# An encoder's dilated-attention mixer: wide transposes for keys and queries, and a seven-product unit in four of its six projection pairs

## The chip, the cores and the metric

The kernel runs on one core of a Trainium2 chip. The metric is the device time of one execution in microseconds, the median of three runs. TensorE (PE) multiplies matrices; VectorE (DVE), ScalarE (ACT) and GpSimd (POOL) do the elementwise work; SyncE (SP) issues most transfers.

## The reference

A bidirectional encoder of two layers over 256 positions of width 2048, all in float32. Each layer is a token mixer and a gated MLP with a depthwise convolution. The first layer's mixer is grouped-query attention. The second layer's mixer, which the change touches, is this (shortened):

```python
def mixer_b(h, w_qkv, w_o, rel_bias):
    qkv = (h @ w_qkv).reshape(b, s, n_g, 3, hg, HEAD_DIM)      # 3 groups, q/k/v, 8 heads of 128
    for g, (window, dil) in enumerate(((128, 1), (512, 4), (2048, 16))):
        o, lz = dilated_group(qkv[:, :, g, 0], qkv[:, :, g, 1], qkv[:, :, g, 2],
                              rel_bias[:, g * hg:(g + 1) * hg], window, dil)
        ...                                 # softmax(q k^T / sqrt(128) + bias) v in the window
    wts = softmax(stack(log_zs), axis=0)    # the groups share the weight of each position
    y = concatenate([wts[g] * outs[g] for g in range(3)], axis=2)
    return y @ w_o
```

So there are 18 projections of 256 x 2048 by 2048 x 512: three groups, each with keys, queries and values, in two halves of four heads.

## The kernel before

**Products.** A weight matrix is packed in blocks of 512 columns and in four chunks of 512 rows. Every float32 product is three TensorE products of parts in the format float32r: high by high, high by low, low by high. `feed` handles one chunk: it loads two weight tiles of 512 KB through SyncE's queue, ScalarE rounds each to a high part (line 144), VectorE takes the difference as the low part (line 145), and TensorE does 24 products of 128 x 128 by 128 x 512 (lines 132 to 134) into two accumulators, one for each 128 positions. `project` feeds the four chunks. There are four buffers for high and for low parts, and these two operations are issued ahead of other work (`tc.high_priority(offset=AHEAD)`).

**The unit.** `fast_unit` takes one chunk for two column blocks at once. Two chunks by plain `feed` are 48 products. The unit treats them as a 2 x 2 by 2 x 2 block product by Strassen's scheme (in Winograd's form): seven block products of 2 x 3 matmuls, 42 in all (lines 186 to 188). It needs sums of weight tiles (line 178, in place), roundings and differences of seven tiles (lines 179, 180), four PSUM tiles besides the four accumulators, sums of the activations' blocks prepared before (`sums_begun`, `sums_made`: adds, differences, one rounding), and a fold of the partial results afterwards (a copy on ScalarE, eight adds and subtractions on VectorE). The gated MLP uses it in `up_pair` for four pairs of a gate and a value block of each layer, in the order `UP_ORDER`: three chunks of the gate side, the unit, three chunks of the value side.

**The second mixer.** For each half `hf` and group `g` the loop projects keys, then queries; then, for the half, the three value blocks. The rest runs beside the projections as generators. `start` puts one into the list `pending`, which `step` resumes once in each half chunk, first come first served; generators in the list `beside` are resumed at the other places. `k_gen` and `s_gen` write the projected keys and queries, scaled, to SBUF (`evac_scaled`, line 489) and turn them so that the head dimension lies on the partitions: `heads_T_dve` does this with 16 transposes of 32 x 256 elements on VectorE (`block_T`, line 386). For group 0 the result is split into high and low parts. Then come four score steps: products, bias, maximum, exponential. `value_stage` turns the probabilities and multiplies by the values; `quad_T` there makes one wide VectorE transpose within 32 x 32 blocks (line 377), and `quad_move` or `quad_place` carries the 16 blocks to their places, on GpSimd (lines 381 and 398) or ScalarE (line 396).

**Order.** The text gives priorities. A scheduler at compile time puts the instructions in each engine's queue, and each engine then works through its queue in order.

Of the kernel before, what the change touches and what calls it, by code (L numbers as in the profile page):

```python
# [14 lines left out]
P = 128  # L15
D = 2048
NT = 256
# [7 lines left out]
AHEAD = 60  # L25
UP = 2, 4, 6, 8
UP_ORDER = (1, 0), (2, 0), (3, 0), (0, None), (1, 1), (2, 1), (3, 1)
NWARM = 11
# [5 lines left out]
def tile_encoder(ctx: ExitStack, tc: tile.TileContext, x, xT, w_a, w_ao, q_gain, k_gain, w_b, w_bo,  # L34
# [355 lines left out]

    def quad_place(o, quad, i0, i1):
        for i in range(i0, i1):
            q, c = QC[i]
            dst, src = o[32 * c:32 * c + 32, :, 32 * q:32 * q + 32], quad[32 * q:32 * q + 32, c]
            if i % 2:
                nc.scalar.activation(dst, src, AF.Copy)
            else:
                nc.gpsimd.tensor_copy(dst, src)  # L398

    def late_transpose(hT, n, g, pool, tag, new_quad):  # L400
# [5 lines left out]
        if n < 3:  # L406
            quad = new_quad()
            for m in range(2):
                quad_T(quad, slice(m, 8, 2), h[:, m, n * 512:(n + 1) * 512])
            yield  # L410
            o = wide_tile(pool, tag)
            for i in range(0, 16, 8):
                quad_place(o, quad, i, i + 8)
# [72 lines left out]
    def evac_scaled(pool, accs, rstd, bufs=2):  # L486
# [3 lines left out]
        return o  # L490

    def ffn(l, hT, ss_in, cw, g_next, last, side=None):
        with tc.tile_pool(name=nm("fpool"), bufs=1) as fp:
# [32 lines left out]
            def folds():  # L526
                return [fp.tile([P, 2, 512], F32, tag=t, name=nm("fold")) for t in ("stg", "st")]

            def new_us():
# [139 lines left out]
            picks = {}  # L669

            def sums(kg, at, r, st):
                yield from sums_begun(kg, r, st)
                sums_made(kg, at, st)

            def sums_begun(kg, r, st, wait=0):
                for _ in range(wait):
                    yield
                hts = [hT[4 * kg + j][:2] for j in range(4)]
                for j, (hi, lo) in enumerate(hts):
                    with tc.issue_after(newest[0].ins):  # L680
                        nc.vector.tensor_tensor(r[:, j], hi.bitcast(F32), lo.bitcast(F32), ALU.add)
                    if j == 1:
                        yield
                v = r.rearrange("p (b j) (m t) -> p b j m t", b=2, m=2)
                st = st.rearrange("p i (j t) -> p i j t", j=2)
                a11, a21, a12, a22 = v[:, 0, :, 0], v[:, 0, :, 1], v[:, 1, :, 0], v[:, 1, :, 1]
                yield
                for o, x, y in ((0, a21, a22), (2, a21, a11), (1, a11, st[:, 0]), (3, a12, st[:, 1])):
                    nc.vector.tensor_tensor(st[:, o], x, y, ALU.subtract)
                yield  # L690

            def sums_made(kg, at, st):
                hts = [hT[4 * kg + j][:2] for j in range(4)]
                own = [pair_slot(at + 2 * i, [P, 4, 2, P], F32R, "s") for i in range(2)]
                split_in_order(*own, st.rearrange("p i (j t) -> p i j t", j=2))
                pick = {q: tuple(tuple(hts[b + j][i][:, m * P:(m + 1) * P] for j in range(2)) for i in range(2))
                        for q, b, m in ((1, 0, 0), (2, 2, 0), (4, 2, 1))}
                for q, i in ((5, 0), (6, 1), (7, 2), (3, 3)):
                    pick[q] = own[0][:, i], own[1][:, i]
                picks[kg] = pick  # L700

            def up_pair(p, order, gate_done):
                (a2, a4), (a3, a8) = new_acc(), new_acc()
                acc, begun = {2: a2, 3: a3, 4: a4, 8: a8}, set()
                sides, ns = ((a2, a4), (a3, a8)), (p, NPAIR + p)
                tt = nc.vector.tensor_tensor
                for i, (kg, side) in enumerate(order):
                    later = {s for _, s in order[i + 1:]}
                    if side is None:
                        acc.update({q: ps_tile() for q in (1, 5, 6, 7)})  # L710
                        end = [q for q, s in ((1, None), (5, None), (6, None), (7, None), (2, 0), (4, 0), (3, 1))
                               if not later & {None, s}]
                        fast_unit(acc, picks[kg], *(w_up[l][n, kg] for n in ns), begun, end, None)
                    else:
                        mine = ((2, 4), (3, 8))[side]
                        feed(sides[side], hT, kg, w_up[l][ns[side], kg], not begun.issuperset(mine),
                             not later & {side, None}, begun=[m for m in range(2) if mine[m] in begun])
                        begun.update(mine)
                    if 0 in begun or not begun >= {1, 2} or later & {0, None}:
                        continue  # L720
                    begun.add(0)
                    a, t = junk(), fp.tile([P, 2, 512], F32, tag="st", name=nm("fold"))
                    v, w = t[:, 0], t[:, 1]
                    nc.scalar.activation(a, acc[1], AF.Copy)
                    with tc.issue_after(newest[0].ins):
                        tt(v, acc[6], a, ALU.subtract)
                        tt(w, acc[7], v, ALU.add)
                        tt(a2, a2, a, ALU.add)
                        tt(a4, a4, w, ALU.subtract)
                    gate_done((a2, a4))  # L730
                    tt(v, acc[5], v, ALU.add)
                    tt(w, acc[5], w, ALU.add)
                tt(a3, a3, v, ALU.add)
                tt(a8, a8, w, ALU.add)
                return a3, a8

            kgs = list(range(4))
            ready = set()
            for hf, (p0, p1) in enumerate(HALVES):
# [5 lines left out]
                for p in range(p0, p1):  # L745
# [12 lines left out]

                    first = partial(sums, 0, 16, cg, cv)
                    if p == p0 and hf == 1:  # L760
                        sums_made(0, 16, early[1])
                    if p == 0:
                        va = project2(w_up[l], 0, NPAIR, hT, kgs, 1, gate_done, None, (), [first])
                    elif p in UP:
                        va = up_pair(p, UP_ORDER, gate_done)
# [92 lines left out]
                if hf == 0:  # L858
                    for ns in (0, 1), (2, 3):
                        if ns[0] == 2:  # L860
                            early = [fp.tile([P, 4, NT], F32, tag=t, name=nm(t)) for t in ("cg", "cv")]
                            start(sums_begun(0, *early, 4))
                        pair(wd, ns, slots, both[0] + both[3] + [(4, 0)] + f0 + [(4, 1), (5, 0)] + f1 + [(5, 1)], spot, folds,
# [383 lines left out]
    def mixer_b(hT, ss_in):  # L1247
        with tc.tile_pool(name="bpool", bufs=1) as bp:
# [14 lines left out]
            def biases(hf, g):  # L1263
# [12 lines left out]
                return [bt[:, None, i, ::-1].to_broadcast([P, 2, P]) for i in range(4)]  # L1276

            cw, turn = load_taps(1)
            allp = slice(None)
            for hf in range(2):  # L1280
# [4 lines left out]
                e = small.tile([P, 3, 8], F32, tag="e", name=nm("e"))  # L1285

                def k_gen(accs, kT):
                    ks = evac_scaled(bp, accs, rstd)
                    yield
                    yield  # L1290
                    yield from heads_T_dve(kT, ks, bp, "vl")

                def s_gen(g, accs, kT, bts, nmx=nmx, lsum=lsum, nmv=nmv, probs=probs, e=e):
                    qs = evac_scaled(bp, accs, rstd)
                    qT = pair_tile(bp, [P, 4, NT], "qT", 1, g > 0)
                    yield
                    yield
                    yield from heads_T_dve(qT, qs, bp, "vl")
                    W = NT if g == 0 else P
# [42 lines left out]
                def value_stage(hf=hf, probs=probs, e=e, vs=vs):  # L1342
# [17 lines left out]
                    def place(quad, n):  # L1360
                        o = wide_tile(bp, ("kTh", "kTl", "qTh", "qTl")[n])
                        if hf == 1 and n > 1:
                            quad_place(o, quad, 0, 16)
                        else:
                            quad_move(o, quad)
# [81 lines left out]
            def own(kg):  # L1447
                return pair_tile(bp, [P, 4, NT], "qT" if kg else "kT")

            def tmp():  # L1450
                return bp.tile([P, 4, NT], F32, tag="pT", name=nm("tmp"), bufs=2)

# [98 lines left out]
```

## Time and profile before

| | |
|---|---|
| median of three runs | 2230.33 us (2229.9 to 2230.64) |
| profiled execution | 2230.45 us, span 2228.6 us |
| TensorE busy | 2214.0 us, 9957 matmuls |
| VectorE, ScalarE, GpSimd busy | 1834.4, 1474.9, 481.0 us |
| keys, queries and values of the second mixer | 966.3 to 1382.4 us of the span |
| one projection of it | about 22 to 25 us |

All times in profile rows are microseconds from the start of the span unless they are marked otherwise. In the timeline a row is: start, duration, engine, line, operation, tiles written and read, count, and in brackets the idle time before it with what ended it. In a group row the count is followed by busy time, the mean of one in nanoseconds, and the idle time before them. In the table by stretch each engine has its busy time and its number of instructions; PEclk is the granted TensorE clock. Matmuls overlap, so the pace is the distance between their starts. The stages of the second mixer begin at 966.3 (keys, half 0, group 0), 988.0 (queries), 1011.2, 1035.6 (group 1), 1058.1, 1081.2 (group 2), 1103.5 (values), and for half 1 at 1173.9, 1199.5, 1221.2, 1245.2, 1267.7, 1290.8 and 1313.1.

### The profile page before, as it was taken

Reading aid. Unit: us, or ns where it says so; the run is one execution under the profiler, and the core shown is the slowest. Engines: PE = TensorE matmul, PEld = TensorE weight load, DVE = VectorE, ACT = ScalarE, POOL = GpSimd, SP = SyncE. Lnnn points to the kernel's source line nnn. Section 1 sums busy time; section 2 is a strip of 40 time slices with the busy share of each in tenths; the row PEclk is TensorE's granted clock in tenths of the full one; section 3 lists DMA queues with packets and bytes.
Section 4 is the critical chain, followed back from the end, with each engine's and each line's share of the span. In section 5 each row is a group of like instructions: output and inputs, shape, how many; then the busy total and the mean of one; then the engine's idle time right before and its main releaser. Section 6 shows DMA issues by size and latency. Waiting matters only on the chain.

```text
span 2228.6 us, 28901 instructions
## 1 busy us (share of the span) xinstructions
PE 2214.0 (99%) x9957; PEld 1833.5 (82%) x9957; DVE 1834.4 (82%) x2385; ACT 1474.9 (66%) x2214; POOL 481.0 (22%) x697
## 2 busy tenths in 40 slices
PE   9999999999999999999999999999999999999998
PEld 7888888888888888888888888888888888888887
DVE  6877669899897887968886878588798998879887
ACT  7667677787457777665455456566777865678764
POOL 3343222321002221040053006003222300112211
PEclk9999999999999999999999999999999999999999
DMA  8565655656656566665556565656555656656654
GB/s 302 193 211 188 217 189 188 201 189 196 204 182 221 184 206 197 198 189 197 187 185 199 178 192 170 205 184 213 189 192 196 198 198 198 214 164 217 222 194 142
DMA packets 126179, 439.59 MB, mean 197 GB/s; under 512 B 14408, under 2 KB 18248, under 8 KB 126032
## 3 DMA queue, kind: packets, MB, share of 16 engines
q1 hardware_dynamic: 123056, 429.05, 58.4%
q0 software_dynamic: 2688, 8.39, 1.5%
q8 instruction: 78, 1.28, 0.2%
q14 instruction: 69, 0.57, 0.1%
q10 hardware_dynamic: 288, 0.30, 0.0%
HBM read 432.34 MB, written 5.34 MB: 196 GB/s over the span
## 4 chain that ended last, share of the span: by engine, by line
PE 53%; DVE 1%; issue 1%; POOL 1%; DMA 1%; ACT 0%; POOLq 0%; DVEq 0%; ACTq 0%
PE acc L133 15%; PE acc L134 15%; PE acc L132 15%; PE ps L187 1%; PE ps L186 1%; PE ps L188 1%; PE acc L187 1%; PE acc L186 1%; PE acc L188 1%; DMA raw<-in_w_b_dram 1%; DVE wl L145 1%; DVE tT L386 1%; POOL wide L398 0%; PE ps L1394 0%; PE ps L339 0%
## 5 line engine op out<-in xcount | busy, mean ns | idle before, releaser
L145 DVE TENSOR_TENSOR wl<-raw,wh 128x1024 fp32r<-128x1024 f32 (+1 forms) x716 | 878.6, 1236 | 250.9 <-ACT wh L144 244.4
L144 ACT ACTIVATE wh<-raw 128x1024 fp32r<-128x1024 f32 (+1 forms) x716 | 745.4, 1047 | 411.3 <-PE acc L134 309.0
L133 PE MATMUL acc<-wl,xh 128*128 128x512 f32 x2048 | 798.7, 390 | 1.8 <-DVE wl L145 1.7
L132 PE MATMUL acc<-wh,xh 128*128 128x512 f32 x2048 | 799.0, 390 | 0.4 <-ACT wh L144 0.4
L134 PE MATMUL acc<-wh,xh 128*128 128x512 f32 x2048 | 797.0, 389 | 0.0
L133 PEld LDWEIGHTS acc<-wl,xh 128*128 128x128 f32 x2048 | 384.7, 188 | 84.4 <-DVE wl L145 6.2
L132 PEld LDWEIGHTS acc<-wh,xh 128*128 128x128 f32 x2048 | 384.7, 188 | 79.9 <-ACT wh L144 0.9
L134 PEld LDWEIGHTS acc<-wh,xh 128*128 128x128 f32 x2048 | 384.5, 188 | 79.4
L561 POOL COPY u<-quad 32x256 f32<-32x256 f32 x352 | 235.0, 668 | 704.7 <-DVE quad L377 686.7
L133 PE MATMUL acc<-wl,a 128*128 128x512 f32 x720 | 280.5, 390 | 0.7 <-DVE wl L145 0.7
L132 PE MATMUL acc<-wh,a 128*128 128x512 f32 x720 | 280.9, 390 | 0.0
L134 PE MATMUL acc<-wh,a 128*128 128x512 f32 x720 | 280.1, 389 | 0.0
L179 ACT ACTIVATE wh<-raw 128x1024 fp32r<-128x1024 f32 x112 | 118.9, 1061 | 108.9 <-PE acc L134 92.1
L561 ACT ACTIVATE u<-quad 32x256 f32<-32x256 f32 x352 | 147.9, 420 | 22.0 <-DVE quad L377 17.5
L133 PEld LDWEIGHTS acc<-wl,a 128*128 128x128 f32 x720 | 135.2, 188 | 29.1 <-DVE wl L145 1.7
L134 PEld LDWEIGHTS acc<-wh,a 128*128 128x128 f32 x720 | 135.1, 188 | 28.2 <-DVE a L328 0.2
L132 PEld LDWEIGHTS acc<-wh,a 128*128 128x128 f32 x720 | 135.2, 188 | 27.6
L180 DVE TENSOR_TENSOR wl<-raw,wh 128x1024 fp32r<-128x1024 f32 x112 | 133.7, 1219 | 4.3 <-ACT wh L179 3.5
L381 POOL COPY wide<-quad 32x256 f32<-32x256 f32 x133 | 89.8, 675 | 169.3 <-DVE quad L377 159.8
L489 ACT ACTIVATE stg<-acc,rstd 128x512 f32<-128x512 f32 x122 | 82.1, 683 | 33.2 <-PE acc L134 25.3
L398 POOL COPY wide<-quad 32x256 f32<-32x256 f32 x88 | 53.2, 605 | 234.6 <-DVE quad L377 167.5
L549 DVE SCALAR_TENSOR_TENSOR cg<-u,cw,cg 128x256 f32<-128x256 f32 x176 | 79.3, 501 | 0.1
(310 smaller groups left out, 2256.7 us busy)
## 6 DMA issues: line engine op xcount, KB each, us to landing
raw<-in_w_up_dram SPq DMA_DIRECT2D x352, 512.0 KB, 4.6
raw<-in_w_down_dram SPq DMA_DIRECT2D x176, 512.0 KB, 4.6
raw<-in_w_b_dram SPq DMA_DIRECT2D x144, 512.0 KB, 4.4
raw<-in_w_bo_dram SPq DMA_DIRECT2D x48, 512.0 KB, 4.3
raw<-in_w_a_dram SPq DMA_DIRECT2D x40, 512.0 KB, 4.9
raw<-in_w_ao_dram SPq DMA_DIRECT2D x32, 512.0 KB, 4.6
raw<-in_w_a_dram SPq DMA_DIRECT2D x16, 256.0 KB, 5.8
there<-quad POOLq DMA_DIRECT2D x6, 512.0 KB, 3.8
```

What stands on the lines that cost most here:

```text
L132: nc.tensor.matmul(accs[m], xh, wh[:, j, :], start=st, stop=False)
L133: nc.tensor.matmul(accs[m], xh, wl[:, j, :], start=False, stop=False)
L134: nc.tensor.matmul(accs[m], xl, wh[:, j, :], start=False, stop=sp)
L144: nc.scalar.activation(wh[:, c], r[:, c], AF.Copy)
L145: newest[0] = nc.vector.tensor_tensor(wl[:, c], r[:, c], wh[:, c].bitcast(F32), ALU.subtract)
L179: nc.scalar.activation(wh, r, AF.Copy)
L180: newest[0] = nc.vector.tensor_tensor(wl, r, wh.bitcast(F32), ALU.subtract)
L381: nc.gpsimd.tensor_copy(o[32 * c:32 * c + 32, :, 32 * q:32 * q + 32], quad[32 * q:32 * q + 32, c])
L398: nc.gpsimd.tensor_copy(dst, src)
L489: evac[0] = nc.scalar.activation(o[:, m, :], accs[m], AF.Copy, scale=rstd[:, m:m + 1])
L549: nc.vector.scalar_tensor_tensor(cj, halves(flat[:, j, o:o + NT])[:, ::-1], tap(n, j, i), cj, ALU.mult, ALU.add)
L561: put(u[32 * c:32 * c + 32, :, :, 32 * q:32 * q + 32], quad[32 * q:32 * q + 32, c].rearrange("p (j m) t -> p j m t", m=2))
```

## The change

Keys and queries of all six pairs are turned by two wide transposes on VectorE and 16 block moves, six of them on GpSimd and ten on ScalarE (`heads`), in place of 16 block transposes on VectorE. In four pairs, groups 1 and 2 of both halves, the key and the query projection become one `up_pair` of six plain chunks and one unit for chunk 0. Three of them use `UP_ORDER`; half 1, group 1 uses `MIX_ORDER`, in which two query chunks come before the unit and one after it. The sums of chunk 0 are prepared in each half beside the query projection of group 0. The key generator of such a pair starts when the unit has been folded, and is resumed from `beside`. During a pair, each third weight tile is loaded into another idle buffer, as the MLP does. The routines `sums`, `sums_begun`, `sums_made` and `up_pair` move out of `ffn` and take their operands as arguments.

```diff
+MIX = (0, 1), (0, 2), (1, 1), (1, 2)
+MIX_ORDER = (1, 0), (2, 0), (3, 0), (1, 1), (2, 1), (0, None), (3, 1)
+EVEN, HEADS_POOL = range(0, 16, 2), range(0, 16, 3)
...
-    def quad_place(o, quad, i0, i1):
-        for i in range(i0, i1):
+    def quad_place(o, quad, which, pool):
+        for i in which:
             q, c = QC[i]
             dst, src = o[32 * c:32 * c + 32, :, 32 * q:32 * q + 32], quad[32 * q:32 * q + 32, c]
-            if i % 2:
+            if i in pool:
+                nc.gpsimd.tensor_copy(dst, src)
+            else:
                 nc.scalar.activation(dst, src, AF.Copy)
-            else:
-                nc.gpsimd.tensor_copy(dst, src)
...
+    def up_pair(w, ns, lhs, order, picks, junk, fold_tile, first_done):
...
+                def heads(o, s):
+                    hi, lo = o
+                    t = hi if lo is None else bp.tile([P, 4, NT], F32, tag="vl", name=nm("tT"))
+                    tv, quad = t.rearrange("p j (m t) -> p (j m) t", m=2), quad_tile(bp, "pT", 2)
+                    for m in range(2):
+                        quad_T(quad, slice(m, 8, 2), s[:, m])
+                    quad_place(tv, quad, HEADS_POOL, HEADS_POOL)
+                    yield
+                    quad_place(tv, quad, [i for i in range(16) if i not in HEADS_POOL], ())
+                    if lo is not None:
+                        yield
+                        yield
+                        split(hi, lo, t)
+
                 def k_gen(accs, kT):
                     ks = evac_scaled(bp, accs, rstd)
                     yield
-                    yield
-                    yield from heads_T_dve(kT, ks, bp, "vl")
+                    yield from heads(kT, ks)
...
                     qT = pair_tile(bp, [P, 4, NT], "qT", 1, g > 0)
                     yield
-                    yield
-                    yield from heads_T_dve(qT, qs, bp, "vl")
+                    yield from heads(qT, qs)
+                    if g > 0:
+                        yield
+                        yield
...
                 for g in range(3):
                     bts = biases(hf, g)
-                    ka = project(w_b, 6 * g + 2 + hf, hT, kgs)
+                    ns = 6 * g + 2 + hf, 6 * g + hf
+                    if (hf, g) in MIX:
+                        kTs = []
+
+                        def k_done(accs, g=g, kTs=kTs):
+                            kTs.append(pair_tile(bp, [P, 4, NT], "kT", 1, g > 0))
+                            gen = k_gen(accs, kTs[0])
+                            next(gen)
+                            beside.append(gen)
+
+                        extra[0] = ((hpool, ["a0", "a1"]), (hpool, ["a6", "a7"]), (bp, ["e0", "e1"]))[hf * g]
+                        qa = up_pair(w_b, ns, hT, MIX_ORDER if (hf, g) == (1, 1) else UP_ORDER, picks, junk, fold_tile, k_done)
+                        extra[0] = None
+                        start(s_gen(g, qa, kTs[0], bts))
+                        continue
+                    ka = project(w_b, ns[0], hT, kgs)
                     kT = pair_tile(bp, [P, 4, NT], "kT", 1, g > 0)
                     start(k_gen(ka, kT))
-                    start(s_gen(g, project(w_b, 6 * g + hf, hT, kgs), kT, bts))
+                    if g == 0:
+                        beside.append(sums(hT, 0, 20, tmp(), tmp(), picks))
+                    start(s_gen(g, project(w_b, ns[1], hT, kgs), kT, bts))
```

More of the change, by code (lines that the diff above doesn't have):

```diff
@@ L412, in late_transpose @@
             for i in range(0, 16, 8):
-                quad_place(o, quad, i, i + 8)
+                quad_place(o, quad, range(i, i + 8), EVEN)
                 yield
@@ new lines, in sums_made @@
+    def sums_made(lhs, kg, at, st, picks):
+        own = [pair_slot(at + 2 * i, [P, 4, 2, P], F32R, "s") for i in range(2)]
+        split_in_order(*own, st.rearrange("p i (j t) -> p i j t", j=2))
+        pick = {q: tuple(tuple(lhs[4 * kg + b + j][i][:, m * P:(m + 1) * P] for j in range(2)) for i in range(2))
+                for q, b, m in ((1, 0, 0), (2, 2, 0), (4, 2, 1))}
+        for q, i in ((5, 0), (6, 1), (7, 2), (3, 3)):
+            pick[q] = own[0][:, i], own[1][:, i]
+        picks[kg] = pick
@@ new lines, in sums @@
+    def sums(lhs, kg, at, r, st, picks):
+        yield from sums_begun(lhs, kg, r, st)
+        sums_made(lhs, kg, at, st, picks)
+    def up_pair(w, ns, lhs, order, picks, junk, fold_tile, first_done):
+        (a2, a4), (a3, a8) = new_acc(), new_acc()
+        acc, begun = {2: a2, 3: a3, 4: a4, 8: a8}, set()
+        sides = (a2, a4), (a3, a8)
+        tt = nc.vector.tensor_tensor
+        for i, (kg, side) in enumerate(order):
+            later = {s for _, s in order[i + 1:]}
+            if side is None:
+                acc.update({q: ps_tile() for q in (1, 5, 6, 7)})
+                end = [q for q, s in ((1, None), (5, None), (6, None), (7, None), (2, 0), (4, 0), (3, 1))
+                       if not later & {None, s}]
+                fast_unit(acc, picks[kg], w[ns[0], kg], w[ns[1], kg], begun, end, None)
+            else:
+                mine = ((2, 4), (3, 8))[side]
+                feed(sides[side], lhs, kg, w[ns[side], kg], not begun.issuperset(mine),
+                     not later & {side, None}, begun=[m for m in range(2) if mine[m] in begun])
+                begun.update(mine)
+            if 0 in begun or not begun >= {1, 2} or later & {0, None}:
+                continue
+            begun.add(0)
+            a, t = junk(), fold_tile()
+            v, w_ = t[:, 0], t[:, 1]
+            nc.scalar.activation(a, acc[1], AF.Copy)
+            with tc.issue_after(newest[0].ins):
+                tt(v, acc[6], a, ALU.subtract)
+                tt(w_, acc[7], v, ALU.add)
+                tt(a2, a2, a, ALU.add)
+                tt(a4, a4, w_, ALU.subtract)
+            first_done((a2, a4))
+            tt(v, acc[5], v, ALU.add)
+            tt(w_, acc[5], w_, ALU.add)
+        tt(a3, a3, v, ALU.add)
+        tt(a8, a8, w_, ALU.add)
+        return a3, a8
@@ L702, in up_pair @@
[L702 to L735, printed above, removed]
@@ L1362, in place @@
                         if hf == 1 and n > 1:
[L1363 removed]
+                            quad_place(o, quad, range(16), EVEN)
                         else:
```

62 lines of the change are left out of this document (28 added, 34 removed).

## The prediction

> **What bounds the kernel now.** I read the page's busy shares first, then the stretch of the second mixer's key, query and value products in the table by stretch, then TensorE's order of time.
>
> ```profile
> span 2228.6 us, 28901 instructions
> PE 2214.0 (99%) x9957; PEld 1833.5 (82%) x9957; DVE 1834.4 (82%) x2385; ACT 1474.9 (66%) x2214; POOL 481.0 (22%) x697
> ```
> ```profile
> core 0: us, PE busy (x) PEld busy (x) DVE busy (x) ACT busy (x) POOL busy (x), PEclk, DMA share, GB/s
> 966.30:1382.40 416.10, 415.12 (x1918) 345.75 (x1916) 332.14 (x510) 218.17 (x328) 92.30 (x132) 1.00 0.61 190
> 988.00:1011.20 23.20, 22.41 (x98) 17.88 (x98) 17.91 (x26) 10.98 (x13) 0.00 (x0) 1.00 0.63 208
> 1011.20:1035.60 24.40, 24.21 (x115) 20.21 (x114) 21.02 (x30) 14.30 (x22) 0.00 (x0) 1.00 0.63 215
> ...
> 1267.70:1290.80 23.10, 23.10 (x110) 19.31 (x108) 18.20 (x28) 11.89 (x20) 0.00 (x0) 1.00 0.60 191
> ```
> TensorE is the bound. In the 416.10 us that the change touches it is idle for 0.98 us, at full granted clock, and all of that lies in two stages of the first half: 0.79 us while group 0's queries are projected (988.0 to 1011.2) and 0.19 us in the stage after. So a product that is taken away shortens the end by its pace, unless a new wait takes its place. The pace is the distance between starts, since a busy time holds the overlap:
>
> ```profile
> 966.29 0.39 PE L132 MATMUL acc<-wh,xh 128*128 128x512 f32 x1
> ...
> 974.22 0.39 PE L134 MATMUL acc<-wh,xh 128*128 128x512 f32 x1
> ```
> These are the first and the last of 36 plain products in a row: 7.93 us over 35 distances, 0.2266 us each.
>
> **The change, part by part.** *Fewer products.* A key projection and a query projection each feed four chunks of 24 products. For four pairs of the six, chunk 0 of both, 48 products, becomes a unit of seven block products with 2 x 3 matmuls each, 42. That is 6 x 4 = 24 matmuls less, 24 x 0.2266 = **5.44 us less** on TensorE. The same routine runs in the gated MLP now; one of its units, first and last of its 42 starts:
>
> ```profile
> 746.79 0.39 PE L186 MATMUL ps<-wh,xh 128*128 128x512 f32 x1
> ...
> 756.15 0.39 PE L188 MATMUL acc<-wh,xh 128*128 128x512 f32 x1
> ...
> 763.18 0.67 ACT L489 ACTIVATE stg<-acc,rstd 128x512 f32<-128x512 f32 x1
> ```
> 41 distances at 0.2266 would be 9.29 us, it took 9.36: 0.07 us of waiting. Four such units: **+0.3 us**. I price them by this row because the order of loads, the buffers and the rounding are the same code.
>
> *Vector, scalar and GpSimd work.* None of these is the bound, but each can become late.
>
> ```profile
> 966.30:1382.40 416.10, 83.65 (x192) 1.00 0.61 190
> ```
> ```profile
> L180 DVE TENSOR_TENSOR wl<-raw,wh 128x1024 fp32r<-128x1024 f32 x112 | 133.7, 1219 | 4.3 <-ACT wh L179 3.5
> L179 ACT ACTIVATE wh<-raw 128x1024 fp32r<-128x1024 f32 x112 | 118.9, 1061 | 108.9 <-PE acc L134 92.1 <-PE ps L188 6.9 <-issue 3.0
> L381 POOL COPY wide<-quad 32x256 f32<-32x256 f32 x133 | 89.8, 675 | 169.3 <-DVE quad L377 159.8 <-DVE xh L334 3.0 <-DVE tot L453 1.1
> L377 DVE STREAM_TRANSPOSE quad<-stg 128x512 f32<-128x512 f32 x88 | 59.3, 694 | 8.9 <-ACT stg L489 8.8
> L178 DVE TENSOR_TENSOR raw<-raw,raw 128x1024 f32<-128x1024 f32 x46 | 57.4, 1247 | 1.1
> L396 ACT ACTIVATE wide<-quad 32x256 f32<-32x256 f32 x88 | 36.6, 416 | 3.1 <-DVE quad L377 1.1 <-DVE xh L334 0.8
> L637 DVE TENSOR_TENSOR st<-cv,st 128x256 f32<-128x256 f32 x16 | 9.7, 605 | 0.0
> L681 DVE TENSOR_TENSOR cg<-xh 128x256 f32<-128x256 f32 x16 | 5.9, 418 | 0.0
> L727 DVE TENSOR_TENSOR fold<-ps,fold 128x512 f32<-128x512 f32 x8 | 5.5, 682 | 0.0
> L724 ACT ACTIVATE junk<-ps 128x512 f32<-128x512 f32 x8 | 4.6, 580 | 0.0
> ```
> The row above these is line 386 alone in the stretch: VectorE's 192 block turns, 83.65 us, all removed. In their place it does 12 x 2 wide turns at 0.694 (16.7 us); in each unit three more weight differences at 1.219 and four weight sums at 1.247 (8.65, four times 34.6); eight folds at 0.682 a pair (21.8); and for each half the sums of chunk 0, four adds at 0.418, four differences at 0.605, one rounding priced as L180 (5.3, twice 10.6). Together 83.7: VectorE's total stays at 332 us, 80%. It moves, though: a pair with a unit has 2.9 us more, a group 0 pair less. ScalarE gets four times three copies at 1.061 (12.7), four at 0.580 (2.3), 12 x 10 block moves at 0.416 (49.9) and two roundings (2.1), so 218 becomes 285 us, 69% of some 411. GpSimd gets 12 x 6 moves at 0.675, 48.6 us, where it is empty now. All this lies beside TensorE and costs nothing by its amount; by its place there are three terms.
>
> *The accumulator at (half 1, group 1).* This pair's own order puts the unit sixth of seven, so one chunk of 24 products is all that lies between it and the next pair, which begins in the two accumulators that the keys leave. Its first product into the second one comes 24 + 3 starts after the unit's last, 27 x 0.2266 = 6.12 us. When that accumulator is emptied, the MLP shows: in the row at 763.18 above, 763.85 - 756.15 = 7.70 us after the last start; the quickest of eight units:
>
> ```profile
> 1713.81 0.39 PE L188 MATMUL acc<-wh,xh 128*128 128x512 f32 x1
> ...
> 1717.92 0.67 ACT L489 ACTIVATE stg<-acc,rstd 128x512 f32<-128x512 f32 x1
> ```
> 1718.59 - 1713.81 = 4.78 us. So 0 to 1.6 us of waiting, and I take **+0.5 us**, since the middle of the two (6.2) lies on the border. The other three pairs have three chunks behind the unit, over 16 us: nothing. Who waits here is TensorE's whole queue.
>
> *The score's place.* Scores stand in TensorE's queue between chunks, and the generator's resumptions fix where. Before, the first score comes at the sixth resumption, now at the fifth, one half chunk (12 x 0.2266 = 2.72 us) sooner.
>
> ```profile
> 1014.65 2.22 DVE L386 STREAM_TRANSPOSE tT<-stg 32x256 f32<-32x256 f32 x5
> 1223.68 2.22 DVE L386 STREAM_TRANSPOSE tT<-stg 32x256 f32<-32x256 f32 x5
> ```
> ```profile
> 1027.52 0.28 PE L341 MATMUL ps<-kTh,qTh 128*128 128x256 f32 x1
> ```
> After the boundary at 1011.2 the first turn starts 3.45 us later, at the boundary 1221.2 2.48 us later. Now follow two wide turns with a weight difference between (2.61), ten moves on ScalarE with two weight copies among them (6.28; GpSimd's six take 4.05 beside it), then for group 0 rounding, 1.06 + 1.22. Low parts stand at 14.6 and 13.6 us; the score's third product, which reads them, at 16.32 - 2.72 + 0.23 = 13.8. One place is 0.8 us late, the other on time. Groups 1 and 2 have no rounding but two folds (1.36) first: 12.7 to 13.7 against 13.6. I take **+0.8 us**; the ends are 0 and, at all six places, the second rival.
>
> *What goes.* The 0.98 us of idle TensorE above stand in the two stages whose block turns disappear. In the first VectorE's 16 turns (7.0) become two wide ones and the sums (6.7), so its amount hardly falls; but a weight difference now waits behind one operation of at most 0.7 us instead of five turns in a row (2.22 us, row above). Between 0 and -1.0 I take **-1.0 us**, the later wait being priced already in the term before.
>
> *Queues.* The number and size of weight loads stay, so SyncE's queue costs nothing; a unit keeps four loaded tiles longer, as the MLP's does. GpSimd's queue holds bias loads that wait:
>
> ```profile
> 1085.35 0.75 POOL L1275 DMA_DIRECT2D btg<-scr  x1 [101.26 <-DVE lg L1312]
> ```
> This load belongs to the second half, a hundred microseconds on, and has been brought ahead of the moves that start at 1136: the queue's order follows readiness and not the text. Head moves behind it would wait, but those of that stage fall before 1070 and after 1095. I price it at nothing; if one set of moves stood behind it, some 15 us.
>
> Sum: -5.44 + 0.3 + 0.5 + 0.8 - 1.0 = **-4.8 us**. The profiled execution took 2230.45 us with a span of 2228.6; the median of the three runs is 2230.33. From the median I get 2225.5 us. No change means within 0.2%, 4.5 us, about what a measurement of this kernel can tell.
>
> **Rivals.** *Given back in small waits (0.24).* Three units follow directly on two scores, whose reading and maximum VectorE does there:
>
> ```profile
> L1312 DVE SCALAR_TENSOR_TENSOR lg<-ps,bt 128x512 f32<-128x512 f32 x8 | 5.5, 690 | 5.8 <-PE ps L343 5.8
> L1313 DVE TENSOR_REDUCE nmx<-lg 128x2 f32<-128x512 f32 x8 | 5.4, 676 | 0.1
> ```
> ```profile
> 362.00:371.40 9.40, 9.40 (x43) 7.62 (x43) 9.33 (x10) 8.25 (x10) 0.00 (x0) 1.00 0.36 114
> ```
> For it: inside an MLP unit VectorE works 9.33 of 9.40 us, with no room, and one score's 1.37 us there could make TensorE wait that long. Three times is +4.1 at most, so 2229.6 us. Against: weight work is issued ahead of everything, and VectorE's lead of four buffers carried all the MLP's units.
>
> *The heads come late everywhere (0.14, slower).* The moves use two in-order queues that also serve weights and exponentials. If at all six score places the last move lands later than I reckon, TensorE waits there: w us each gives -4.8 - 0.8 + 6w. It decides from w = 0.9, and is slower by over 0.2% from w = 1.7; with 2 us, 2230.3 + 6.4 = 2236.7 us. For it: TensorE takes its queue in order, and the margins above are under 1 us. Against: ScalarE has 31% left.
>
> *A lock between VectorE and GpSimd (0.04).* Weight differences without and with GpSimd's copies beside them, and those copies (windows 1300 to 1340, then 1346 to 1370):
>
> ```profile
> L145 DVE TENSOR_TENSOR wl<-raw,wh 128x1024 fp32r<-128x1024 f32 x15 | 18.3, 1223 | 4.1 <-ACT wh L144 3.9
> ```
> ```profile
> L145 DVE TENSOR_TENSOR wl<-raw,wh 128x1024 fp32r<-128x1024 f32 x10 | 13.3, 1355 | 1.7 <-ACT wh L144 1.7
> ```
> ```profile
> L381 POOL COPY wide<-quad 32x256 f32<-32x256 f32 x31 | 22.9, 738 | 152.3 <-DVE quad L377 151.0
> ```
> Were a whole copy's time taken from VectorE, a set of six would cost it 6 x 0.675 = 4.05 us, where it has 23.10 - 18.20 = 4.9 in a stage, less half of 2.9: 3.4. Short by 0.65 in each of twelve sets, +7.8, so 2233.3 us, still within 0.2%. The rows speak against it: with copies running all through, a difference took 0.13 us longer, not 0.7. The Trainium skill, "SBUF — State Buffer", section "Who interferes with whom", says that a VectorE instruction with two SBUF inputs and a GpSimd instruction that reads SBUF exclude each other, the later one blocking fully; by that rule the sum would be this rival's, and the trace shows a fraction of it.
>
> That the unit is not reached, or the products stay, the code excludes.
>
> **How the numbers follow.** The forecast has 0.58: waits that sum to less than 1 us. The small waits and the lock, 0.28, end within 0.2%. The late heads have 0.14. The forecast's own ends are -5.44 - 1.0 = -6.4 with no new wait (2223.9) and the 0.2% border (2225.9); the range reaches over the small waits to 2232.0 and down to 2223.5.
>
> **What would show it.** 9933 matmuls instead of 9957; no line 386 in the second mixer; units of 42 starts in 9.3 to 9.5 us; the stretch about 411.3 us; TensorE idle in it under 2 us. A wait at the start of (half 1, group 2) for the keys' evacuation shows that term; waits of score products for moves or roundings of 1.7 us or more each, at most places, would prove me wrong, as would units of over 10.5 us.

## The result, and the profile after

The changed kernel took 2226.40 us, the median of 20 runs, against 2230.36 us of the kernel before in 20 runs beside it: 3.96 us less, a ratio of 0.9981 with a 95% interval of 0.9974 to 0.9988. It is faster, by just under the 0.2% that I had set as the border, and by less than the 4.8 us that I had forecast (2225.5); the range holds it.

The profiled execution took 2227.28 us, 0.9 above that median. In rows of this kernel and of the runs further down the line numbers are a little higher than before: plain products stand on lines 135 to 137, a unit's on 189 to 191, weight copies on 147 and 182, weight differences on 148 and 183, sums of weight tiles on 181, block moves on 399 (GpSimd) and 401 (ScalarE), evacuations on 492, score products on 344 to 346 (group 0) and 342. First the head of the page, then the stretch of the second mixer's projections in the table by stretch:

```profile
span 2225.5 us, 28992 instructions
PE 2209.3 (99%) x9933; PEld 1829.3 (82%) x9933; DVE 1821.1 (82%) x2295; ACT 1537.2 (69%) x2352; POOL 530.8 (24%) x769
```
```profile
966.20:1377.90 411.70, 409.98 (x1894) 341.24 (x1893) 320.28 (x421) 280.77 (x466) 141.12 (x204) 1.00 0.60 190
```
There are 24 matmuls less. ScalarE has 62.6 us more in the stretch (67.0 forecast), GpSimd 48.8 (48.6 forecast), VectorE 11.9 less (0 forecast, with each duration counted in full, though consecutive instructions overlap a little). How long the stretch is, I read from the third product of a plain chunk, its first and last start, before and after:

```profile
L134 PE MATMUL acc<-wh,xh x576: 388/389/397, 966.7 to 1382.2; 128*128 128x512 f32 x192
```
```profile
L137 PE MATMUL acc<-wh,xh x512: 388/389/398, 966.7 to 1377.7; 128*128 128x512 f32 x171
```
415.5 us became 411.0: 4.4 less, on unrounded starts (415.45 and 411.01). That is the change's own result, known from one profile each. The whole span is only 3.1 us shorter, since one unit in the last MLP's down-projection lost over a microsecond in this execution (below). All that TensorE waited for in the stretch, in the list of waits from 960 to 1385:

```profile
PE ps L190 <- DVE wl L183: 1.7, 3, 0.9
```
Only units wait, for weight differences, and most of it in one of them. Starts of the last unit (half 1, group 2), its two waits, and its last start:

```profile
1279.47 0.48 PE L189 MATMUL ps<-wh,xh 128*128 128x512 f32 x1
...
1284.94 0.50 PE L190 MATMUL ps<-wl,s 128*128 128x512 f32 x1 [0.91 <-DVE wl L183]
...
1287.21 0.49 PE L190 MATMUL ps<-wl,s 128*128 128x512 f32 x1 [0.61 <-DVE wl L183]
...
1290.99 0.39 PE L191 MATMUL acc<-wh,xh 128*128 128x512 f32 x1
```
This unit took 11.52 us; the three before it took 9.84, 9.39 and 9.29, where 9.29 is a unit without waits. ScalarE's and VectorE's order of time just before it suggest why it was late:

```profile
1263.66 4.26 ACT L401 ACTIVATE kT<-quad 32x256 f32<-32x256 f32 x10
1267.95 1.27 ACT L492 ACTIVATE stg<-acc,rstd 128x512 f32<-128x512 f32 x2
1269.10 2.00 ACT L147 ACTIVATE wh<-raw 128x1024 fp32r<-128x1024 f32 x2
1271.13 4.27 ACT L401 ACTIVATE qT<-quad 32x256 f32<-32x256 f32 x10
1275.42 2.96 ACT L182 ACTIVATE wh<-raw 128x1024 fp32r<-128x1024 f32 x3
```
```profile
1276.52 1.23 DVE L183 TENSOR_TENSOR wl<-raw,wh 128x1024 fp32r<-128x1024 f32 x1 [3.68 <-ACT wh L182]
```
ScalarE moves ten blocks of keys and ten of queries within 12 us, because this pair's predecessor has its unit sixth, so that its keys are turned only at the border between the two pairs. The unit's weight copies stand behind these moves in ScalarE's queue, VectorE sits idle for 3.68 us, and its lead is gone when TensorE arrives.

### The profile page after: what moved, and what is told of

Its sections match the earlier page's. It is cut to its first block, busy times and chain, and to the rows that moved or that the text cites. A ratio compares the mean times of both kernels' runs of the same rounds, so it can differ in the third digit from the quotient of the medians.

```text
span 2225.5 us, 28992 instructions
## 1 busy us (share of the span) xinstructions
PE 2209.3 (99%) x9933; PEld 1829.3 (82%) x9933; DVE 1821.1 (82%) x2295; ACT 1537.2 (69%) x2352; POOL 530.8 (24%) x769
## 4 chain that ended last, share of the span: by engine, by line
PE 90%; DVE 4%; ACT 2%; DMA 1%; issue 1%; POOL 1%; SPq 0%; DVEq 0%; POOLq 0%; ACTq 0%
PE acc L136 26%; PE acc L135 26%; PE acc L137 26%; PE ps L190 2%; PE ps L191 2%; PE ps L189 2%; PE acc L190 1%; PE acc L191 1%; PE acc L189 1%; DVE wl L148 1%; ACT wh L147 1%; DVE wl L183 1%; DMA raw<-in_w_down_dram 1%; DMA raw<-in_w_a_dram 1%; DVE raw L181 0%
## 5 line engine op out<-in xcount | busy, mean ns | idle before, releaser
L148 DVE TENSOR_TENSOR wl<-raw,wh 128x1024 fp32r<-128x1024 f32 (+1 forms) x700 | 858.5, 1237 | 263.8 <-ACT wh L147 259.0
L147 ACT ACTIVATE wh<-raw 128x1024 fp32r<-128x1024 f32 (+1 forms) x700 | 727.3, 1046 | 345.7 <-PE acc L137 239.4
L136 PE MATMUL acc<-wl,xh 128*128 128x512 f32 x1984 | 774.4, 390 | 1.4 <-DVE wl L148 1.4
L135 PE MATMUL acc<-wh,xh 128*128 128x512 f32 x1984 | 774.3, 391 | 0.0
L137 PE MATMUL acc<-wh,xh 128*128 128x512 f32 x1984 | 772.6, 389 | 0.0
L136 PEld LDWEIGHTS acc<-wl,xh 128*128 128x128 f32 x1984 | 372.8, 188 | 81.3 <-DVE wl L148 6.1
L137 PEld LDWEIGHTS acc<-wh,xh 128*128 128x128 f32 x1984 | 372.6, 188 | 77.4
L135 PEld LDWEIGHTS acc<-wh,xh 128*128 128x128 f32 x1984 | 372.8, 188 | 76.6 <-ACT wh L147 0.3
L182 ACT ACTIVATE wh<-raw 128x1024 fp32r<-128x1024 f32 x140 | 148.2, 1060 | 122.6 <-PE acc L137 100.5
L183 DVE TENSOR_TENSOR wl<-raw,wh 128x1024 fp32r<-128x1024 f32 x140 | 167.2, 1220 | 9.2 <-ACT wh L182 8.7
L380 DVE STREAM_TRANSPOSE quad<-stg 128x512 f32<-128x512 f32 x112 | 75.7, 698 | 13.1 <-ACT stg L492 12.7
```

What stands on the lines that cost most here:

```text
L135: nc.tensor.matmul(accs[m], xh, wh[:, j, :], start=st, stop=False)
L136: nc.tensor.matmul(accs[m], xh, wl[:, j, :], start=False, stop=False)
L137: nc.tensor.matmul(accs[m], xl, wh[:, j, :], start=False, stop=sp)
L147: nc.scalar.activation(wh[:, c], r[:, c], AF.Copy)
L148: newest[0] = nc.vector.tensor_tensor(wl[:, c], r[:, c], wh[:, c].bitcast(F32), ALU.subtract)
L182: nc.scalar.activation(wh, r, AF.Copy)
```

## The experiments

The theory was this crowding on ScalarE. The rival was my own from the prediction, score work on VectorE within the unit. "Stretch" is always the distance in the row of line 137 above; units are named by their length from first to last start. A border is the place where one pair or projection ends and the next begins. The scores of group 0 are wide (512 columns), those of the other groups narrow (256).

**The changed kernel again** (no edit).

> The changed kernel, unaltered, a second time. Its first profile lost 1.4 us in a unit of the last MLP's down-projection (10.68 us instead of 9.29), outside the changed stretch, and the stretch itself, from the first to the last plain product of the second mixer's projections, took 411.0 us (415.5 before). If the loss in the MLP is that run's accident (a late weight load), it is gone here and the stretch is again 411.0 within 0.3 us; if it belongs to the change, that unit is again over 10.3 us. Units of the four pairs, in their order: 9.8, 9.4, 9.3, 11.5 us, if these waits are the kernel's and not the run's. Time 3 to 5 us below the kernel before.

2226.49 us, ratio 0.9984 (0.9976 to 0.9993). Stretch 411.8, 0.8 longer than in the first profile, part of it a wait of 0.37 us in one plain chunk. So much can two profiles of one kernel differ, and a smaller difference of stretches shows nothing by itself. Units 9.82, 9.39, 9.29, 11.48 us: these waits belong to the kernel. The MLP's loss belongs to the kernel too, by the sign that I had set: its unit took 10.35 us again, and another 10.28.

**The usual order for half 1, group 1 as well.**

```diff
-up_pair(w_b, ns, hT, MIX_ORDER if (hf, g) == (1, 1) else UP_ORDER, picks, ...)
+up_pair(w_b, ns, hT, UP_ORDER, picks, ...)
```


> Half 1, group 1 uses the order of the three other pairs, so its keys are turned three chunks before its queries and not just before them. Theory (ScalarE's block moves): the 11.5 us unit of half 1, group 2 was late because ScalarE carried ten key moves and ten query moves, 8.5 us, within 12 us just before it and made the unit's weight copies late; with the keys' moves gone from there that unit falls to 9.8 us or less, the stretch to 409.0 to 409.8 us, though half 1, group 1's own unit, which now follows two wide scores, rises from 9.3 to about 9.8. Rival (VectorE's score work inside the unit): the unit of half 1, group 2 has the same two narrow scores before it and stays at 11 us or more, and half 1, group 1's rises too: stretch 411.3 or more.

2224.23 us, ratio 0.9976 (0.9967 to 0.9985).

```profile
L137 PE MATMUL acc<-wh,xh x512: 388/389/397, 963.9 to 1373.6; 128*128 128x512 f32 x171
```
Stretch 409.7. The last unit fell from 11.52 to 9.87, as the theory says; its two narrow scores are still there. The unit of group 1 took 9.32, although it now follows two wide scores; I had expected 9.8. The unit's first copies show the difference:

```profile
1267.02 4.26 ACT L401 ACTIVATE qT<-quad 32x256 f32<-32x256 f32 x10 [0.31 <-DVE quad L380]
1271.30 2.01 ACT L182 ACTIVATE wh<-raw 128x1024 fp32r<-128x1024 f32 x2
```
The unit starts at 1277.10, 5.8 us after its first weight copy; in the changed kernel it was 1279.47 - 1275.42 = 4.05.

**The unit sixth of seven in all four pairs** (`MIX_ORDER` for each).

> All four pairs use the order with the unit sixth of seven, behind all four scores of the group before. Both the theory (block moves on ScalarE) and the rival (score work on VectorE) expect units of 9.3 to 9.5 us everywhere, since neither the moves nor the scores stand before the unit any more, and a stretch of 408.2 to 409 us. They differ in what may go wrong at the border of two pairs: keys and queries are turned together at all four borders, so if the moves alone were enough to make TensorE late, new waits would appear in the plain chunks after the borders (1 us or more each); by the theory a plain chunk asks for half as many copies per time and shows none. A third thing could show, the accumulators' wait that the prediction priced at 0.5: a wait of the first chunk of half 0, group 2 and half 1, group 2 for the keys' evacuation.

2226.00 us, ratio 0.9983 (0.9974 to 0.9992). All four units took 9.29 us, and yet the stretch was 411.6:

```profile
PE acc L135 <- ACT stg L492: 1.7, 1, 1.7
PE ps L342 <- ACT qT L401: 0.5, 1, 0.5
```
The first row is the accumulators' wait, at the border into half 0, group 2 (at 1056.8): the keys' evacuation ended 8.2 us after the unit's last start, held up by a weight copy that waited 2.8 us for its load in front of it. The second is a score that waited for the queries' moves. Both are terms of the prediction, in a place where I had not put them.

**The transposes alone.** `MIX = ()` and no sums.

> The wide transposes and block moves in all six pairs, no unit in any and no sums for it. 9957 matmuls as before. By my steps the stretch is the one of before less its idle time: 415.5 - 1.0 to - 1.8 = 413.7 to 414.5 us, and the time 0.5 to 2 us below the kernel before. If the block moves made TensorE late by themselves, it is 415.5 or more. The difference to the changed kernel's 411.0 is what four units bring: 5.44 less 2.9 of waiting inside them = 2.5 to 3.5 us.

2228.62 us, ratio 0.9991 (0.9983 to 1.0000).

```profile
L137 PE MATMUL acc<-wh,xh x576: 389/389/402, 964.2 to 1378.1; 128*128 128x512 f32 x192
```
Stretch 413.95, and the list of waits is empty for TensorE. So the turning removes the idle time that there was, 1.5 us by these two profiles and by the medians alike, and adds none. The ratio's interval reaches 1, so the whole runs alone do not tell this kernel from the one before.

**The units alone**, with the 16 block turns on VectorE as before, for keys and for queries.

```diff
-                    yield from heads(kT, ks)
+                    yield
+                    yield from heads_T_dve(kT, ks, bp, "vl")
...
-                    yield from heads(qT, qs)
-                    if g > 0:
-                        yield
-                        yield
+                    yield
+                    yield from heads_T_dve(qT, qs, bp, "vl")
```


> The four units and their sums, but keys and queries turned by 16 block transposes on VectorE as before. 9933 matmuls. A pair with a unit then has 14 us more VectorE work than before the change (four weight sums, three more differences, eight folds) and saves none of the 11.2 us of turns: some 54 of 46 us in half 0, group 1, so VectorE would bind there. If the wide turns were needed to make room for the unit, the units take 11 us or more, other chunks wait too, and the stretch is 418 us or more (415.5 before); if VectorE's load did not matter, it is 410 to 412 as in the changed kernel.

2262.20 us, ratio 1.0142 (1.0128 to 1.0156), stretch 445.0. The waits in the stretch:

```profile
PE ps L342 <- DVE qT L389: 20.0, 4, 8.7
PE acc L190 <- DVE wl L183: 4.0, 3, 2.8
PE ps L346 <- DVE qTl L331: 1.9, 1, 1.9
PE acc L136 <- DVE wl L148: 1.2, 2, 0.7
```
27 us of waits, and the larger part is not for the units' weight work, as I had expected, but for the turns. Two of the four waits for turns, 7.8 and 8.7 us, stand inside the units of group 2, which thereby took 21.0 and 25.5 us: the old turning has one resumption more, so that the first scores come behind the twelfth of a unit's 42 products. The last turns come behind the unit's own work on VectorE:

```profile
1086.12 1.22 DVE L183 TENSOR_TENSOR wl<-raw,wh 128x1024 fp32r<-128x1024 f32 x1
1087.37 1.79 DVE L389 STREAM_TRANSPOSE qT<-stg 32x256 f32<-32x256 f32 x4
```
```profile
1089.22 0.58 PE L342 MATMUL ps<-kT,qT 128*128 128x128 f32 x1 [7.81 <-DVE qT L389]
```
TensorE's granted clock fell to 0.50 for a few us within both these units too; the stretch has 20 products at the slow pace of about 0.43 us, which cost 4 us more. How much of the loss is VectorE's load and how much the later place of the scores, this run does not separate. The two halves of the change belong together: 1.5 us for the turns alone, a loss of 32 us for the units alone.

**All moves on ScalarE** (`HEADS_POOL = ()`).

> All 16 block moves of each turn on ScalarE, none on GpSimd; the rest is the changed kernel. ScalarE gets 2.5 us more in each of twelve turns. If late copies on ScalarE made the unit of half 1, group 2 late, that unit, 11.5 us now, grows by 2 to 5 us to 13.5 to 16.5, since ten or twelve of the added moves stand before it, and the others, whose moves lie two chunks or more ahead of the unit, by less than 1: stretch 413 to 416 us. If score work on VectorE made it late, it stays at 11 to 12 and the stretch within 1 us of 411.0. If GpSimd's copies held VectorE's differences by the lock that the prediction weighed, differences get shorter here and the stretch falls.

2241.93 us, ratio 1.0056 (1.0042 to 1.0070), stretch 427.1. Units 11.14, 11.72, 9.29 and 12.48: the first two are later by 1.3 and 2.3 us, where I had expected less than 1, and the last by 1.0, where the theory asked for 2 to 5. Scores wait as well, the longest of them (2.8 us) right before the last unit, which gave that unit's copies time:

```profile
PE ps L342 <- ACT qT L401: 5.4, 4, 2.8
...
PE acc L189 <- ACT wh L182: 1.5, 2, 0.9
PE ps L189 <- ACT wh L182: 1.3, 2, 0.6
```
Here units wait for ScalarE itself, which speaks for the theory's cause, though not for its size: 2.5 us more of moves in each turn cost 16 us, spread over units and scores, and my 413 to 416 us was far too small. Weight differences on VectorE got hardly shorter without the moves on GpSimd, 1.24 us in the mean against 1.25.

**All moves on GpSimd** (`HEADS_POOL = range(16)`).

> All 16 block moves on GpSimd, none on ScalarE. ScalarE is free: by the theory of late copies the unit of half 1, group 2 falls to under 10 us. But a turn's moves now take 16 x 0.73 = 11.7 us one after the other, against 5.4 us, so the moves should land about 13 us after the border for queries alone, and the first score, at 13.6, would wait at group 0, whose rounding follows (2 us each, two places), and at half 1, group 2, where the keys' moves stand in front of the queries' (8 us or more). Stretch 415 to 425 us: the prediction's slower rival made real. If GpSimd and VectorE exclude each other for a whole copy, weight differences beside the moves take 1.9 us instead of 1.36 and waits spread to plain chunks as well.

2249.08 us, ratio 1.0086 (1.0072 to 1.0100), stretch 432.3. The last unit fell to 9.41, as the theory says. A score's wait of 9.1 us, a little more than a chunk before it, would have hidden a late copy too; but without it, and without the slow products behind it (below), the unit would have begun at about 1289 (an estimate: 1301.14 less 9.15 and 2.8), still 9 us after its first weight copy at 1280.23, where the changed kernel had 4.05. Three of the four units kept to 9.3 to 9.4. The first took 13.0, with waits of 2.5 and 0.6 us: VectorE stood idle for 6.2 us before it at the queries' low part, which waits for the moves on GpSimd, and the unit's weight work stands behind that in its queue. The rest are scores:

```profile
PE ps L342 <- POOL qT L399: 13.5, 4, 9.1
```
9.1 us of it at half 1, group 2, where the keys' moves stand in front of the queries' in GpSimd's queue:

```profile
1272.39 15.31 POOL L399 COPY kT<-quad 32x256 f32<-32x256 f32 x16 [35.26 <-DVE quad L380]
1287.76 6.92 POOL L399 COPY qT<-quad 32x256 f32<-32x256 f32 x16
```
The same 16 moves took 15.3 us beside VectorE's weight differences and 6.9 us while VectorE was idle; the last section takes this up. Behind that wait TensorE also ran at half its clock for 14 products, 0.427 us from start to start in place of 0.227, or 2.8 us more:

```profile
1294.70:1300.60 5.90, 5.87 (x16) 4.81 (x17) 3.20 (x4) 0.88 (x4) 0.00 (x0) 0.50 0.00 0
```
The granted clock of 0.50 is the last figure but two. This is the slower rival made real: of the three divisions tried in this order of chunks, only the shared one cost TensorE no wait at a score. Weight differences beside the copies took 1.31 us in the mean of 81, not the 1.9 that I had put for a lock.

**Group 1 in the usual order, group 2 with the unit sixth.**

> Group 1's pairs in the usual order, group 2's with the unit sixth, behind all scores and just before the values. From the runs so far: the unit of half 0, group 1 keeps 9.8 us, the three others 9.3; what lies behind group 2's pairs is a value projection with no unit, and the accumulators' wait seen at the border into half 0, group 2 (1.7 us) does not come, because the value projection's border showed none with this order. Stretch 409.7 - 0.6 - 0.1 = 409.0 us, 6.4 below the kernel before; time 2223 to 2225 us. If the accumulators' wait comes at the borders into the values instead, 410.5 to 412.

2225.24 us, ratio 0.9977 (0.9967 to 0.9987), stretch 409.8. Units 9.82, 9.29, 9.32, 9.29 as expected, but the accumulators' wait came at the border into half 1's values (0.5 us). The stretch is 0.8 longer than expected, and no better than with the usual order everywhere.

**The unit fifth of seven in all four pairs.**

```diff
-MIX_ORDER = (1, 0), (2, 0), (3, 0), (1, 1), (2, 1), (0, None), (3, 1)
+MIX_ORDER = (1, 0), (2, 0), (3, 0), (1, 1), (0, None), (2, 1), (3, 1)
...
-up_pair(w_b, ns, hT, MIX_ORDER if (hf, g) == (1, 1) else UP_ORDER, picks, ...)
+up_pair(w_b, ns, hT, MIX_ORDER, picks, ...)
```


> All four pairs with the unit fifth of seven: three key chunks, one query chunk, the unit, two query chunks. By the runs so far this meets all three waits: the four scores of the group before are placed by the end of the fourth chunk, so no score work stands in the unit (9.8 in half 0, group 1 with the unit fourth, 9.3 with it sixth); the keys are turned two chunks before the queries, so ScalarE's moves do not crowd the next pair's copies (11.5 when they did); and two chunks, 10.9 us, lie between the unit and the next use of the keys' accumulators, which were free 4.8 to 8.2 us after a unit. Units 9.3 to 9.5 us, no accumulator wait, stretch 408.3 to 409.0 us, 6.5 to 7 below the kernel before; time 2223 to 2224.5 us. If the last score's reading falls into the unit, units of 9.5 to 9.9 and a stretch of 409 to 410, no better than with the unit fourth everywhere.

2223.75 us, ratio 0.9975 (0.9966 to 0.9984).

```profile
L137 PE MATMUL acc<-wh,xh x512: 389/389/397, 966.5 to 1375.1; 128*128 128x512 f32 x171
```
```profile
PE ps L190 <- DVE wl L183: 0.2, 1, 0.2
```
Stretch 408.6, 6.85 below the kernel before, with one wait of 0.2 us left. One unit took 9.87, the others 9.32 to 9.39. In the profile this is the shortest stretch of all; by whole runs it cannot be told from the usual order everywhere.

## Why the prediction was right or wrong

The measured gain, 3.96 us, is 0.8 of the forecast one, and that is in part luck: the units cost 2.6 us more than their term, and the three terms for waits and idle time came out 1.8 us better than theirs. By the border that I had set, the time lies on the side of the rival of small waits, and one unit of 11.52 us is past the 10.5 that I had named as a sign of being wrong. The waits in the stretch sum to 1.7 us, where the forecast had said less than 1.

- **Fewer products, -5.44.** Right: 9933 matmuls, at the same pace.
- **The units, +0.3.** This is the step that failed. The four took 40.04 us where 37.16 is the least: +2.9. I priced them by a unit of the MLP "because the order of loads, the buffers and the rounding are the same code", but what goes ahead of them in ScalarE's queue is not. I had added up ScalarE's 49.9 us of moves and set them aside as 69% of the stretch, and never asked which twelve of these microseconds come just before a unit. The first rival had the right place and the wrong engine: it is worth 0.5 us at half 0, group 1 (9.84, and 9.29 in the run with the unit sixth, behind all scores), where four operations on wide scores stand among VectorE's work for the unit, while of the 2.2 us at the last unit 1.65 come from ScalarE: they went away with the keys' moves, with the scores still in place. The 0.6 that stayed is the size of the scores' share, but no run took the scores away alone.
- **The accumulator at (half 1, group 1), +0.5.** No wait there. The evacuation ended 4.8 us after the unit, the quicker end of my bounds. The mechanism is real: 1.7 us at the border of half 0, group 2 when that pair's predecessor got the same order, 0.5 us at another border.
- **The score's place, +0.8.** No wait. The distance from the border to the first turn, 3.45 us in the row I used, held a weight copy that waited for its load; in the changed kernel the first wide turn began 0.2 us after the border. The low part was there 2.9 us before the score:

```profile
1019.38 1.22 DVE L331 TENSOR_TENSOR qTl<-tT,qTh 128x1024 fp32r<-128x1024 f32 x1
```
```profile
1023.49 0.28 PE L344 MATMUL ps<-kTh,qTh 128*128 128x256 f32 x1
```
- **What goes, -1.0.** Larger: the transposes alone made the stretch 1.5 us shorter, more than the idle time of 0.98. Idle time understates a wait: the one of 0.28 us made two distances of 0.67 and 0.34 us between starts, where 0.227 each is the pace, so it cost 0.55; the three together cost 1.8 by the same count.
- **The queues.** Right for GpSimd: a bias load did come between two sets of moves (1095.66) and delayed nobody.
- **The slower rival.** It didn't come here, but the two runs that give one engine all the moves show how near it was. The run with all on GpSimd pays 0.8 to 2.6 us at three places, where I had named 2 us at each of six, and 9.1 at a fourth.
- **The lock.** The price, 0.65 us of VectorE's time for each set of moves, was wrong, and so was the reading of the rows: they do not speak against an exclusion; I had looked at VectorE's side alone. The exclusion is there, and it is mostly the copies that wait (last section). None of the units' 28 differences had a copy beside it, so it does not explain the units' waits.

Measured: -5.44 + 2.87 - 1.5 = -4.1 for the stretch, against -4.44 in the profile; 0.4 us are not assigned, less than two profiles of one kernel differ by. Outside the changed code something is given back, which is why the span fell by 3.1 us only. In both profiles of the changed kernel a unit in the last MLP's down-projection began late:

```profile
1813.09 1.23 DVE L181 TENSOR_TENSOR u<-raw,raw 128x1024 f32<-128x1024 f32 x1 [4.30 <-DMA raw<-in_w_down_dram]
```
```profile
PE acc L190 <- DVE wl L183: 1.0, 1, 1.0
```
VectorE waits there for a weight load, 4.3 and 4.0 us in the two profiles, against 3.04 before; TensorE then lost 1.4 and 1.1 us in the unit. In the kernel with the usual order everywhere the wait was 2.6 us and the unit took no longer than 9.5. Three loads landed after 6.3 to 6.9 us instead of 5.5 to 5.6. Why they are slower in this kernel, I could not find; it stays open.

## What to carry to other kernels

A unit that was free in one stage is priced by its lead: ask what stands ahead of its feeding copies in each in-order queue during the few microseconds before it, not how busy that engine is over the stage. Where a compute-heavy block may sit in a sequence, there are three distances to keep at once: after the neighbour's scores, after the block moves, and far enough ahead of the next use of its accumulators; of the three places tried here, the fourth, the fifth and the sixth of seven, the fifth left the least waiting (0.2 us). An edit that adds work should be tried with and without the edit that makes room for it: neither half predicts the whole.

## What I had not expected of the hardware

GpSimd's copies of 32 x 256 elements took 0.43 us each in the first set of six of the stretch and up to 0.9 in others (2.57 and 5.45 us a set):

```profile
991.27 2.57 POOL L399 COPY tT<-quad 32x256 f32<-32x256 f32 x6 [7.22 <-DVE quad L380]
...
1090.26 5.45 POOL L399 COPY kT<-quad 32x256 f32<-32x256 f32 x6 [27.00 <-DVE quad L380]
```
No run was made for this spread, but the trace shows what goes with it. VectorE was idle during the first set. A single copy mostly takes one of two times. Of the 72 moves of keys and queries on GpSimd, 49 took 0.39 to 0.40 us. The other 23 all began while a weight difference was running on VectorE, and each ended 0.25 to 0.26 us after that difference did: 22 of them took 1.21 to 1.44 us, and one that began near a difference's end took 0.46. One pair, with the short copies on both sides of it:

```profile
1011.59 0.39 POOL L399 COPY tT<-quad 32x256 f32<-32x256 f32 x1 [17.75 <-DVE quad L380]
1011.76 1.30 DVE L148 TENSOR_TENSOR wl<-raw,wh 128x1024 fp32r<-128x1024 f32 x1 [0.24 <-ACT wh L147]
1012.02 1.30 POOL L399 COPY tT<-quad 32x256 f32<-32x256 f32 x1
1013.37 0.39 POOL L399 COPY tT<-quad 32x256 f32<-32x256 f32 x1
```
The difference ran until 1013.06 and the copy until 1013.32. In the run with all moves on GpSimd the same holds for 48 of 192 moves (1.21 to 1.46 us), while 18 that began inside other work of VectorE (folds, the scores' reading and maximum, wide transposes) took 0.39 to 0.40. So a copy that comes during a weight difference waits for its end. The other way round costs little, since the copies are short: in the changed kernel's stretch weight differences with copies beside them took 1.29 us in the mean of 56 (1.45 at most), against 1.22 without (101). That is the exclusion of the prediction's third rival, with the waiting on the other side: VectorE loses at most the rest of one copy, GpSimd up to a whole difference.
